# Two-layer encoder on one core: down-stage raw tiles loaded earlier, bank copies moved behind the second step, per-layer input split in the down stage

## The chip, the core and the metric

The kernel runs on one core of one Trainium2 chip. The core has a matrix engine (TensorE, PE below; its weight loads are listed apart as PEld), three engines for elementwise work (VectorE or DVE, ScalarE or ACT, GpSimd or POOL) and SyncE (SP), whose queue issues most of the loads from memory (POOL issues some too). Each engine works through its own queue in order and waits on semaphores for the others. Matmul results stand in eight PSUM banks. The metric is the time of one execution on the device in microseconds (us).

## The reference

Input is a sequence of 512 positions with 1024 features. There are two layers; the parts that the change touches are the feed-forward half-steps and the per-layer input at the end of a layer:

```python
for i in range(DEPTH):                                   # DEPTH = 2
    h = h + 0.5 * swiglu(rmsnorm(h, norm_ffn1[i]), ffn1_w_gate[i], ffn1_w_up[i], ffn1_w_down[i])
    hn = rmsnorm(h, norm_mix[i])
    h = h + (ab_mixer(hn, ...) if i % 2 == 0 else c_mixer(hn, ...))
    h = h + 0.5 * swiglu(rmsnorm(h, norm_ffn2[i]), ffn2_w_gate[i], ffn2_w_up[i], ffn2_w_down[i])
    gate = sigmoid(rmsnorm(h, norm_ple[i]) @ w_ple_gate[i])
    h = h + gate * (p[i] @ w_ple_proj[i])
return rmsnorm(h, norm_final)

# swiglu(x, w_gate, w_up, w_down) = (silu(x @ w_gate) * (x @ w_up)) @ w_down ; hidden width 2816
```

All of it is float32.

## The kernel before

Activations lie with features on the 128 partitions: `h` is 8 tiles of 128 x 512. Every float32 operand of a product is split into a high part (ACT copies it to a rounded type, line 150) and a low part (DVE, at some places POOL, subtracts, line 151); a product is then three matmuls, high x high, high x low, low x high (`mm3`, lines 175 to 177; in the fast products lines 390 to 392 and 498 to 500). So each weight tile goes through a load (`wr`, `rb` or `tmp` tiles), a split on ACT into `wh`, a split on DVE into `wl`, and the matmuls.

One feed-forward half-step (`ffn`, line 420) runs over 22 chunks of 128 hidden features ("pairs" of a gate and an up product). The first five use plain or half-split products, the other 17 (`pair_fast`) seven half-sized ones that are combined on ACT and DVE (lines 399 to 417, the last being the Silu and the product of gate and up). The result is one `act` tile per chunk, in the list `a`.

Then comes the down projection (`down`, line 458), here called a down stage; there are four, starting at about 240, 878, 1285 and 1857 us. It begins with four chunks in plain form on two `tr` banks (`rx`, lines 515 to 519; 24 matmuls). Their raw weights come through `halved`, which takes `tmp` tiles, issues their loads (line 482) and splits them. The two banks are then copied to `act` tiles (`cx`, lines 520 and 506), and two new `tr` banks `rb` are taken. The remaining 18 chunks go in five steps `s` (lines 569 to 573): `first(s)` into two `mm` banks, `second(s)` into an `mm` and the `ob` bank (12 matmuls each, where a step has two chunks), and from the third step on `fifth(s - 2)` into the `sc` banks. Weight sums of two quarters are made by accumulating loads on POOL's queue (line 489). A second loop (lines 590 to 608) runs the rest (`seventh`, `sixth`, `fourth`), and a third the last quarter and the transposes back to `h` with the splits for the next norm.

The per-layer stage (`ple`, line 1331), at about 1000 and 1979 us, loads the two tiles of `p` and splits them (lines 1336 to 1338, low half on POOL), multiplies the first two chunks of the gate and of `p` (`mm_units` and `inner`), starts the third chunk's gate product `ahead`, and then needs the norm's factor R: sums of squares over the partitions by matmuls with ones (line 233, `stat`), scaled on DVE (line 235), raised to -1/2 on POOL (line 236), spread over the partitions by transposes (line 252) and copied by ACT (line 260). With R, DVE frees the gate banks (line 1372).

What sets the order: the program is written in the order above, and at build time a scheduler turns it into one queue per engine, earlier-written work first where its operands and buffers are to be had. Buffers come from pools with fixed counts: 8 `tmp`, 5 `wr`, 2 `rb`, 4 `wh`, 4 `wl`, 62 `act`; of the PSUM banks 3 `mm`, 2 `sc`, 2 `tr`, 1 `ob`. A load stands in SP's queue until its buffer is free, and everything behind it waits with it. `issue_after(ins)` puts the instructions that it encloses behind `ins` on that engine.

Of the kernel before, what the change touches and what calls it, by code (L numbers as in the profile page):

```python
# [16 lines left out]
T = 512  # L17
D = 1024
KC = D // P
# [15 lines left out]
WHOLE = 4  # L35
# [13 lines left out]
class Trunk:  # L49
# [370 lines left out]
    def ffn(self, i, which, k_next):  # L420


        nc, io = self.nc, self.io
        gu, dn = io[f"gu{which}"], io[f"dn{which}"]
        first = i == 0 and which == 1
        a, y, z, t = [], [None] * KC, [None] * (KC // 2), [None] * (KC // 2)

        kept = io["xT"].rearrange("p c t -> c p t") if first else self.put_away()
        xs, sums = [None] * WHOLE, [None] * K2
        for m in range(NF):  # L430
            if m == NF - 1:
                xs[:LEAD_X] = [self.split_chunk(x, nc.vector) for x in a[:LEAD_X]]
            if m < FRONT:
                r = self.pair_front(gu[i, m], m, first, gu[i, m + 1])
            elif m == FRONT:
                r = self.pair(gu[i, m], y, z)
            else:
                r = self.pair_fast(gu[i, m], y, t)
            a.append(r)
            k = (m - WHOLE) // 2  # L440
            if m > WHOLE and (m - WHOLE) % 2 and k < READY:
                sums[k] = self.inner_sums(*a[m - 1:])
            for c, after in enumerate(SUMS):
                if m == after:
                    y[c], z[c], y[c + KC // 2], t[c] = self.halves(c)
        self.begin_norm(k_next)
        self.down(dn[i], a, xs, sums, kept)

    def inner_sums(self, a, b):

# [4 lines left out]
        tt(s[:, l], s[:, r], b[:, r], op=ALU.add)  # L455
        return s

    def down(self, w, a, xs, sums, kept):

        nc, H = self.nc, T // 2
        l, r = slice(0, H), slice(H, T)
# [10 lines left out]
            nc.sync.dma_start(raw, b[:, u.start * T:u.stop * T])  # L474
            return raw

        def halved(b, u):
            hi = self.wh.tile([P, UNIT], F32R, tag="wh", name=self.nm("wh"))
            lo = self.wl.tile([P, UNIT], F32R, tag="wl", name=self.nm("wl"))
            raws = [self.tmp() for _ in u]  # L480
            for raw, k in zip(raws, u):
                nc.sync.dma_start(raw, b[:, k * T:(k + 1) * T])
            for j, raw in enumerate(raws):
                c = slice(j * T, (j + 1) * T)
                self.split(raw, hi[:, c], lo[:, c])
            return hi, lo
# [16 lines left out]
        def copied(p):  # L503
            out = [self.act() for _ in p]
            for o, x in zip(out, p):
                copy(o, x, AF.Copy)
            return out
# [8 lines left out]
        for u in wide:  # L516
            for k in u:
                xs[k] = xs[k] or self.split_chunk(a[k], nc.vector)
            product(rx, u, halved(right, u), xs, r, True, u.stop == WHOLE)
        cx = copied(rx)  # L520
        rb = [self.tbank(), self.tbank()]

        def summed(s):
            raws[s] = load(b12, units[s])
# [13 lines left out]
        def second(s):  # L538
            u = units[s]
            for k in u:  # L540
                x2[k] = self.split_chunk(B[k], nc.vector)
            product(r2, u, halved(b21, u), x2, l, True)
# [26 lines left out]
        for s in range(n):  # L569
            first(s)  # L570
            second(s)
            if s > 1:
                fifth(s - 2)
        c11, c5 = copied(r1), cx
        summed(0)
        seventh(0)
        ws = [halved(left, u) for u in wide]
# [12 lines left out]
        for s in range(1, n + 2):  # L590
            if s + 1 < n:
                summed(s + 1)
            if s < n:
                seventh(s)
            if s <= n:
                sixth(s - 1)
            if s > 1:
                fourth(s - 2)
            if s in (2, 3):
                u = wide[s - 2]  # L600
                product(r3, u, halved(right, u), xs, l)
            if s == n:
                c2 = copied(r1)
                u3 = [self.act(), self.act()]
                for i in range(2):
                    tt(u3[i], c2[i], rb[i], op=sub)
                for i in range(2):
                    tt(c5[i], c5[i], u3[i], op=sub)
# [722 lines left out]
    def ple(self, i, k_next, regroup):  # L1331

        nc, io = self.nc, self.io
        xg, p = self.xg, []
        for c in range(2):
            raw = self.tmp()
            nc.sync.dma_start(raw, io["pT"][i, :, c, :])
            p.append(self.split_chunk(raw))
        up, ends, first = None, [], []
        for m in range(KC):  # L1340
            self.fetch(self.kept, m)
# [5 lines left out]
            if m == 0:  # L1347
                first = [(u, self.bank(), self.obank()), (self.unit(io["plg"][i, 1]), self.bank(), self.sbank())]

                def inner():  # L1350
                    for j, (_, _, q) in enumerate(first):
                        self.mm_unit(q, tuple(x[:, j * 2 * P:(j + 1) * 2 * P] for x in up), p, True, True)

                self.mm_units([f[1] for f in first], [f[0] for f in first], inner)
                next_u, ahead = self.unit(io["plg"][i, 2]), self.bank()
                self.mm_unit(ahead, next_u, xg, True, True)

            half = k_next == N_NORM - 1 and m == KC - 1
            for x in (slice(0, T // 2), slice(T // 2, T)) if half else (slice(0, T),):
# [215 lines left out]
```

## Time and profile before

| | us |
|---|---|
| median of 3 runs | 2052.09 (2049.68 to 2052.36) |
| the profiled execution, on the device | 2050.14 |
| its span from first to last instruction | 2048.4 |
| PE busy | 2008.8 (98%) |
| DVE busy | 1598.8 (78%) |
| ACT busy | 1127.6 (55%) |
| POOL busy | 280.3 (14%) |

The mean granted clock of PE in that execution is 0.994. Times in the rows of the trace count from the span's start. A row of the order of time gives start, duration, engine, line, operation, output and input names (buffer numbers left out), shapes and count, and in brackets how long the engine had been idle and what it had waited for. A matmul's record lasts longer than the interval to the next one, since they are pipelined.

### The profile page before, as it was taken

Reading aid. Unit: us, or ns where it says so; the run is one execution under the profiler, and the core shown is the slowest. Engines: PE = TensorE matmul, PEld = TensorE weight load, DVE = VectorE, ACT = ScalarE, POOL = GpSimd, SP = SyncE. Lnnn points to the kernel's source line nnn. Section 1 sums busy time; section 2 is a strip of 40 time slices with the busy share of each in tenths; the row PEclk is TensorE's granted clock in tenths of the full one; section 3 lists DMA queues with packets and bytes.
Section 4 is the critical chain, followed back from the end, with each engine's and each line's share of the span. In section 5 each row is a group of like instructions: output and inputs, shape, how many; then the busy total and the mean of one; then the engine's idle time right before and its main releaser. Section 6 shows DMA issues by size and latency. Waiting matters only on the chain.

```text
span 2048.4 us, 33392 instructions
## 1 busy us (share of the span) xinstructions
PE 2008.8 (98%) x12438; PEld 1786.9 (87%) x12438; DVE 1598.8 (78%) x2799; ACT 1127.6 (55%) x1954; POOL 280.3 (14%) x318
## 2 busy tenths in 40 slices
PE   9999999999999999999999999999999999999998
PEld 6999888879788899978788999788888889997876
DVE  8888776798766888885778888858888688888675
ACT  6455555477645455564554555745766445556552
POOL 0001011342212000011120000113000200001212
PEclk9999999999999999999999999999999999999998
DMA  6766698553425466588555665985343446657961
GB/s 196 181 183 183 184 205 219 168 95 82 98 62 175 121 186 177 160 218 209 190 165 129 180 182 160 231 206 182 106 128 99 164 117 172 181 165 203 208 227 42
DMA packets 134963, 334.94 MB, mean 164 GB/s; under 512 B 24592, under 2 KB 32272, under 8 KB 134800
## 3 DMA queue, kind: packets, MB, share of 16 engines
q1 hardware_dynamic: 106944, 245.72, 36.2%
q0 software_dynamic: 27712, 87.05, 24.3%
q8 instruction: 98, 1.61, 0.3%
q14 instruction: 65, 0.53, 0.1%
q10 hardware_dynamic: 144, 0.04, 0.0%
HBM read 304.42 MB, written 17.27 MB: 157 GB/s over the span
## 4 chain that ended last, share of the span: by engine, by line
PE 73%; DVE 3%; issue 2%; ACT 2%; POOL 0%; DVEq 0%; ACTq 0%; POOLq 0%
PE mm L176 5%; PE mm L175 5%; PE mm L177 5%; PE mm L392 5%; PE mm L391 5%; PE mm L390 5%; PE sc L391 2%; PE sc L390 2%; PE sc L392 2%; PE mm L498 2%; PE mm L500 2%; PE mm L499 2%; PE sc L177 2%; PE sc L175 2%; PE sc L176 2%
## 5 line engine op out<-in xcount | busy, mean ns | idle before, releaser
L150 ACT ACTIVATE wh<-wr 128x1024 fp32r<-128x1024 f32 (+2 forms) x435 | 448.1, 1032 | 431.1 <-PE mm L176 61.2
L151 DVE TENSOR_TENSOR wl<-wr,wh 128x1024 fp32r<-128x1024 f32 (+2 forms) x435 | 524.0, 1206 | 153.4 <-ACT wh L150 151.7
L391 PE MATMUL mm<-act,wh 128*128 128x256 f32 x1088 | 307.9, 283 | 0.0
L390 PE MATMUL mm<-act,wh 128*128 128x256 f32 x1088 | 307.9, 283 | 0.0
L392 PE MATMUL mm<-act,wl 128*128 128x256 f32 x1088 | 307.9, 283 | 0.0
L175 PE MATMUL mm<-act,wh 128*128 128x512 f32 (+1 forms) x632 | 248.4, 395 | 1.4 <-ACT wh L150 0.6
L176 PE MATMUL mm<-act,wh 128*128 128x512 f32 (+1 forms) x632 | 247.7, 393 | 0.6 <-DVE act L214 0.6
L177 PE MATMUL mm<-act,wl 128*128 128x512 f32 (+1 forms) x632 | 246.9, 391 | 0.9 <-DVE wl L151 0.9
L390 PEld LDWEIGHTS mm<-act,wh 128*128 128x128 f32 x1088 | 208.8, 192 | 0.2
L391 PEld LDWEIGHTS mm<-act,wh 128*128 128x128 f32 x1088 | 208.9, 192 | 0.2
L392 PEld LDWEIGHTS mm<-act,wl 128*128 128x128 f32 x1088 | 208.9, 192 | 0.0
L390 PE MATMUL sc<-act,wh 128*128 128x256 f32 x544 | 154.0, 283 | 0.0
L391 PE MATMUL sc<-act,wh 128*128 128x256 f32 x544 | 154.0, 283 | 0.0
L392 PE MATMUL sc<-act,wl 128*128 128x256 f32 x544 | 154.0, 283 | 0.0
L368 POOL DMA_DIRECT2D wr<-in_gu_dram x68 | 59.2, 870 | 677.4 <-DMA wr<-in_gu_dram 255.8
L175 PEld LDWEIGHTS mm<-act,wh 128*128 128x128 f32 x632 | 119.2, 189 | 25.2 <-ACT wh L150 1.5
L176 PEld LDWEIGHTS mm<-act,wh 128*128 128x128 f32 x632 | 119.3, 189 | 24.9 <-DVE act L214 3.9
L177 PEld LDWEIGHTS mm<-act,wl 128*128 128x128 f32 x632 | 119.1, 188 | 23.2 <-DVE wl L151 1.9
L489 POOL DMA_DIRECT2D wr<-in_dn_dram x80 | 69.3, 879 | 427.8 <-DVE wl L151 220.0
L151 DVE TENSOR_TENSOR act<-act,act 128x512 fp32r<-128x512 f32 (+1 forms) x176 | 108.2, 632 | 13.4 <-ACT act L150 9.4
L150 ACT ACTIVATE act<-act 128x512 fp32r<-128x512 f32 (+1 forms) x176 | 96.9, 577 | 19.5 <-PE sc L500 8.5
L390 PEld LDWEIGHTS sc<-act,wh 128*128 128x128 f32 x544 | 104.4, 192 | 0.0
(255 smaller groups left out, 4888.8 us busy)
## 6 DMA issues: line engine op xcount, KB each, us to landing
wr<-in_gu_dram SPq DMA_DIRECT2D x176, 512.0 KB, 4.4
wr<-in_gu_dram POOLq DMA_DIRECT2D x68, 512.0 KB, 5.5
wr<-in_dn_dram POOLq DMA_DIRECT2D x64, 512.0 KB, 7.5
tmp<-in_dn_dram SPq DMA_DIRECT2D x120, 256.0 KB, 5.1
rb<-in_gu_dram SPq DMA_DIRECT2D x68, 256.0 KB, 2.5
wr<-in_dn_dram SPq DMA_DIRECT2D x32, 512.0 KB, 4.6
act<-kept SPq DMA_DIRECT2D x56, 256.0 KB, 5.3
wr<-in_qk_ab_dram SPq DMA_DIRECT2D x20, 512.0 KB, 3.8
```

Of the source, the lines that this page charges most:

```text
L150: self.put(self.nc.scalar.activation(hi, src, AF.Copy))
L151: self.put((lo_eng or self.nc.vector).tensor_tensor(lo, src, hi.bitcast(F32), op=ALU.subtract))
L175: mm(out, stat[0], mov[0], start=start, stop=False)
L176: mm(out, stat[0], mov[1], start=False, stop=False)
L177: return mm(out, stat[1], mov[0], start=False, stop=stop)
L368: nc.gpsimd.dma_start(rs, w[:, :UNIT], accum_op=ALU.add)
L390: mm(out, w[0][:, c], xs[k][0][:, x], start=start and k == 0, stop=False, skip_group_check=True)
L391: mm(out, w[0][:, c], xs[k][1][:, x], start=False, stop=False, skip_group_check=True)
L392: mm(out, w[1][:, c], xs[k][0][:, x], start=False, stop=stop and k == half - 1, skip_group_check=True)
L489: nc.gpsimd.dma_start(raw, b[:, u.start * T:u.stop * T], accum_op=ALU.add)
L498: mm(p, xh, wh, start=start and k == 0, stop=False, skip_group_check=True)
L499: mm(p, xh, wl, start=False, stop=False, skip_group_check=True)
```

## The change

In `ffn`, ahead of the last pair, four `tmp` tiles (`begin`) are taken and the loads of the first four raw tiles of the down weights are issued; `halved` uses them in place of its own for the `rx` products. In `down`, the copy of the two `rx` banks moves from right behind their products to behind the second step (`s == 1`), and the two new `tr` banks `rb` are taken behind the copy of `r1`, after the loop. In the second half-step of a layer (`which == 2`), `down` calls `inner` in the second turn of its second loop, which loads and splits both tiles of `p`, now with the low half on DVE; `ple` takes them from there. In `ple`, `ahead` is computed in two halves; the sums over the partitions (`rcol`) stand behind the first half and the spread (`R`) behind the second.

```diff
@@ ffn
             if m == NF - 1:
                 xs[:LEAD_X] = [self.split_chunk(x, nc.vector) for x in a[:LEAD_X]]
+                begin = [self.tmp() for _ in range(WHOLE)]
+                for k, raw in enumerate(begin):
+                    nc.sync.dma_start(raw, dn[i, :, (WHOLE + k) * T:(WHOLE + k + 1) * T])
...
-        self.down(dn[i], a, xs, sums, kept)
+        p = lambda: [self.per_layer(i, c) for c in range(2)]
+        self.down(dn[i], a, xs, sums, begin, kept, p if which == 2 else None)
+
+    def per_layer(self, i, c):
+        raw = self.tmp()
+        self.nc.sync.dma_start(raw, self.io["pT"][i, :, c, :])
+        return self.split_chunk(raw, self.nc.vector)
@@ down
-        def halved(b, u):
+        def halved(b, u, raws=None):
...
-            raws = [self.tmp() for _ in u]
-            for raw, k in zip(raws, u):
-                nc.sync.dma_start(raw, b[:, k * T:(k + 1) * T])
+            if raws is None:
+                raws = [self.tmp() for _ in u]
+                for raw, k in zip(raws, u):
+                    nc.sync.dma_start(raw, b[:, k * T:(k + 1) * T])
...
-            product(rx, u, halved(right, u), xs, r, True, u.stop == WHOLE)
-        cx = copied(rx)
-        rb = [self.tbank(), self.tbank()]
+            product(rx, u, halved(right, u, begin[u.start:u.stop]), xs, r, True, u.stop == WHOLE)
...
             second(s)
+            if s == 1:
+                c5 = copied(rx)
             if s > 1:
                 fifth(s - 2)
-        c11, c5 = copied(r1), cx
+        c11 = copied(r1)
+        rb = [self.tbank(), self.tbank()]
...
             if s > 1:
                 fourth(s - 2)
+            if s == 2 and inner:
+                self.p = inner()
@@ ple
-        xg, p = self.xg, []
-        for c in range(2):
-            raw = self.tmp()
-            nc.sync.dma_start(raw, io["pT"][i, :, c, :])
-            p.append(self.split_chunk(raw))
+        xg, p = self.xg, self.p
...
                 next_u, ahead = self.unit(io["plg"][i, 2]), self.bank()
-                self.mm_unit(ahead, next_u, xg, True, True)
+                self.mm_unit(ahead, next_u, xg, True, True, range(KC // 2))
+                with self.tc.issue_after(self.last_mm.ins):
+                    self.rcol
+                self.mm_unit(ahead, next_u, xg, True, True, range(KC // 2, KC))
+                with self.tc.issue_after(self.last_mm.ins):
+                    self.R
```

In the new file the lines behind `ffn` have moved: 498 to 500 are now 509 to 511, 474, 482, 489 and 506 are 484, 493, 500 and 517, and 1372 is 1387. The queues differ from before at the start of the four down stages, in the second loop of two of them, and in the two `ple` stages; elsewhere they are the same. Three places show how, each in the first stage of its kind.

ACT's queue at the end of the last pair and the start of the down stage, before (L408, L414 and L416 belong to the last pair; `act_463` and `act_559` are the third and fourth chunk of `a`, `act_678`, `act_833` and `act_705` operands of the first step):

```order
L416 ACTIVATE act_2721<-act_2721 128x512
L150 ACTIVATE wh_2830<-tmp_2832 128x512
L150 ACTIVATE wh_2830<-tmp_2833 128x512
L150 ACTIVATE wh_2860<-tmp_2862 128x512
L150 ACTIVATE wh_2898<-wr_2888 128x1024
L150 ACTIVATE wh_2860<-tmp_2863 128x512
L150 ACTIVATE wh_2923<-tmp_2925 128x512
L150 ACTIVATE wh_2923<-tmp_2926 128x512
L150 ACTIVATE wh_2955<-wr_2945 128x1024
L506 ACTIVATE act_2882<-tr_2828 128x512
L506 ACTIVATE act_2883<-tr_2829 128x512
L150 ACTIVATE act_2890<-act_678 128x512
```

and now:

```order
L150 ACTIVATE wh_2838<-tmp_2697 128x512
L150 ACTIVATE wh_2838<-tmp_2698 128x512
L150 ACTIVATE act_2856<-act_463 128x512
L150 ACTIVATE act_2860<-act_559 128x512
L150 ACTIVATE wh_2864<-tmp_2699 128x512
L150 ACTIVATE wh_2864<-tmp_2700 128x512
L150 ACTIVATE act_2884<-act_678 128x512
L408 ACTIVATE tmp_2731<-mm_2726 128x256
L150 ACTIVATE act_2888<-act_833 128x512
L150 ACTIVATE wh_2892<-wr_2882 128x1024
L150 ACTIVATE act_2909<-act_705 128x512
L414 ACTIVATE act_2729<-mm_2726 128x256
```

The splits of the four raw tiles and of the first step's operands stand ahead of the last pair's L408 and L414; the bank copies (now L517) stand 13 rows behind the last one shown. DVE's low halves move in the same way.

SP's queue, as a difference (`wr` and `tmp` loads of `in_dn` are raw down weights, `rb_7683` and `rb_7811` belong to a later half-step):

```order
 L366 DMA rb_7683<-in_gu_dram 128x512
-L474 DMA wr_3075<-in_dn_dram 128x1024
-L474 DMA wr_3156<-in_dn_dram 128x512
+L435 DMA tmp_2697<-in_dn_dram 128x512
+L435 DMA tmp_2698<-in_dn_dram 128x512
+L435 DMA tmp_2699<-in_dn_dram 128x512
+L435 DMA tmp_2700<-in_dn_dram 128x512
+L484 DMA wr_3073<-in_dn_dram 128x1024
+L484 DMA wr_3154<-in_dn_dram 128x512
 L366 DMA rb_7811<-in_gu_dram 128x512
-L482 DMA tmp_2832<-in_dn_dram 128x512
-L482 DMA tmp_2833<-in_dn_dram 128x512
```

The four raw tiles now go ahead of two `wr` loads and an `rb` load that they stood behind.

PE's queue in the first `ple` stage around the statistics, before (`mm_11037` is `ahead`, `sc_11113` the third chunk's product with `p`, `mm_11144` the fourth chunk's gate product):

```order
L177 MATMUL mm_11037<-act_10776,wl_11033 128x512
L233 MATMUL tr_11063<-ones,ssq_10903 128x1 x4
L175 MATMUL sc_11113<-act_10935,wh_10956 128x512
L176 MATMUL sc_11113<-act_10936,wh_10956 128x512
L252 MATMUL tr_11072<-ident,rcol_11069 128x128 x4
L177 MATMUL sc_11113<-act_10935,wl_10957 128x512
```

and now, where the ten rows between the two pieces are more of `mm_11037`:

```order
L177 MATMUL mm_11037<-act_10872,wl_11033 128x512
L233 MATMUL tr_11050<-ones,ssq_10915 128x1 x4
L175 MATMUL mm_11037<-act_10746,wh_11032 128x512
...
L177 MATMUL mm_11037<-act_10788,wl_11033 128x512
L252 MATMUL tr_11072<-ident,rcol_11056 128x128 x4
L175 MATMUL sc_11113<-act_10464,wh_10956 128x512
L176 MATMUL sc_11113<-act_10465,wh_10956 128x512
```

Twelve matmuls of `ahead` now stand between the statistics and the spread; the products of the first two chunks with `p` have moved ahead in the queue, among the matmuls on the first gate chunk.

More of the change, by code (lines that the diff above doesn't have):

```diff
@@ L456, in inner_sums, with down @@
         return s
-    def down(self, w, a, xs, sums, kept):
+    def down(self, w, a, xs, sums, begin, kept, inner):
         nc, H = self.nc, T // 2
```

## The prediction

> **What bounds the kernel now.** I read the totals first, then the waits of TensorE (PE), then the order of time around each wait. Totals, and the two longest lines of the waits (engine and line that waited, what released it, us in total, times, longest):
>
> ```profile
> PE 2008.8 (98%) x12438; PEld 1786.9 (87%) x12438; DVE 1598.8 (78%) x2799; ACT 1127.6 (55%) x1954; POOL 280.3 (14%) x318
> ...
> PE tr L498 <- ACT wh L150: 8.5, 4, 2.1
> PE mm L498 <- ACT act L150: 4.8, 4, 1.2
> ```
>
> PE sets the time: the 2048.4 us span gets shorter only where PE's idle or slow time does. Both waits occur four times, once each at the start of the four down stages. The first down stage, in order of time on PE (start, us, engine, line, what; idle before in brackets):
>
> ```profile
> 237.97 0.28 PE L392 MATMUL mm<-act,wl 128*128 128x256 f32 x1
> 240.37 0.80 PE L498 MATMUL tr<-wh,act 128*128 128x512 f32 x1 [2.12 <-ACT wh L150]
> ...
> 247.01 0.39 PE L499 MATMUL tr<-wl,act 128*128 128x512 f32 x1
> 247.24 0.39 PE L500 MATMUL tr<-wh,act 128*128 128x512 f32 x1
> 248.83 0.50 PE L498 MATMUL mm<-wh,act 128*128 128x512 f32 x1 [1.20 <-ACT act L150]
> ```
>
> A 512-column matmul starts every 0.23 us (247.01 to 247.24) though its record lasts 0.39, and a 256-column one every 0.12; an idle time in brackets therefore leaves out 0.16 us of what a wait costs. The entry costs 240.37 - 237.97 - 0.12 = 2.28 us and the second wait 248.83 - 247.24 - 0.23 = 1.36 us. The 24 matmuls between them run from 240.37 to 247.47, 7.1 us, where 24 x 0.23 = 5.5 would do: 1.6 us more. The stretches (us from the start, busy us of PE, PEld, DVE, ACT, POOL; then granted clock, DMA share, GB/s) say why:
>
> ```profile
> 236.80:240.20 3.40, 1.45 (x13) 1.25 (x11) 1.49 (x3) 1.42 (x3) 0.00 (x0) 1.00 0.94 337
> 240.20:243.61 3.41, 3.24 (x8) 2.46 (x9) 3.41 (x6) 3.41 (x7) 0.00 (x0) 0.50 0.56 180
> ...
> 1281.26:1284.67 3.41, 2.05 (x18) 1.85 (x16) 1.17 (x3) 0.83 (x2) 0.00 (x0) 1.00 0.98 348
> 1284.67:1288.08 3.41, 2.58 (x10) 1.86 (x11) 3.19 (x6) 3.41 (x7) 0.00 (x0) 1.00 0.58 189
> ...
> 1015.03:1018.44 3.41, 1.65 (x13) 1.21 (x12) 1.35 (x2) 0.97 (x1) 2.00 (x1) 1.00 0.13 47
> ...
> 1998.06:2001.47 3.41, 3.41 (x11) 2.51 (x10) 1.09 (x2) 2.51 (x3) 0.00 (x0) 0.50 0.00 0
> ```
>
> After such a wait the clock stands at half for one stretch of 3.41 us, which loses 1.7 us of work. There are five such stretches, the first and the last of which are quoted: three down stages and both `ple` stages. The third down stage (1285) had the same wait but its idle fell over two stretches, PE was busy 2.05 us in the first, and the clock stayed at 1.00; 1.65 us busy in the `ple` was too little.
>
> [...]
>
> **Down stages: what the change does.** Why PE enters late: ScalarE (ACT) and the loads on SP's queue.
>
> ```profile
> 235.41 0.38 ACT L408 ACTIVATE tmp<-mm 128x256 f32<-128x256 f32 x1 [2.38 <-PE mm L392]
> ...
> 239.16 0.63 ACT L416 ACTIVATE act<-act 128x512 f32<-128x512 f32 x1 [0.49 <-DVE act L415]
> 239.70 1.65 ACT L150 ACTIVATE wh<-tmp 128x512 fp32r<-128x512 f32 x3
> ...
> 246.99 1.28 ACT L506 ACTIVATE act<-tr 128x512 f32<-128x512 f32 x2 [1.00 <-PE tr L500]
> 248.16 0.62 ACT L150 ACTIVATE act<-act 128x512 fp32r<-128x512 f32 x1
> ```
>
> ```profile
> 222.67 0.33 SPq L366 DMA_DIRECT2D rb<-in_gu_dram  x1
> 227.39 3.90 SPq L474 DMA_DIRECT2D wr<-in_dn_dram  x2
> 232.75 0.33 SPq L366 DMA_DIRECT2D rb<-in_gu_dram  x1
> 233.13 24.56 SPq L482 DMA_DIRECT2D tmp<-in_dn_dram  x18
> ```
>
> The raw tiles are issued from 233.13, behind two `wr` loads and an `rb` load that wait for buffers, and their splits stand on ACT behind the last pair's Silu (239.16), so `wh` is there only at 240.3. In the new order four raw loads follow the `rb` of 222.67 and are issued at some 223 to 225. One lands in 4.6 us (median):
>
> ```profile
> tmp<-in_dn_dram SPq DMA_DIRECT2D x18, 256.0 KB, 4.6
> ```
>
> Four of them behind each other may take twice that, so they are there by 228 to 233. ACT has room for their four splits (three take 1.65 us, 239.70): it idles 2.38 us before the L408 of 235.41, and the `wh` buffers come free as PE works through the pair. **Entry wait: gone, and with it the slow stretch.** The cover is the time between 233 and PE's need at 238.1; gone, the 2.28 us return at each stage.
>
> The second wait has another cause: the two bank copies (L506, 1.28 us on ACT) stand ahead of the split of `act` that PE needs, and they wait for PE's last `tr` matmul. In the new order both splits of the first step stand ahead of the last pair's L414, and the copies some 25 rows later, where their banks have long been ready. **Second wait: gone.** The moved splits cost L408 little: five of 0.5 us now fill its 2.38 us of idle and may hold it some tenths, and PE needs its bank again only after 12 matmuls, 1.4 us later. The copies' banks are next wanted after all five steps, so holding them is free.
>
> What could be late next is VectorE (DVE), which makes the low half of every split and is full early in the stage:
>
> ```profile
> 900.00:910.00 10.00, 10.00 (x46) 8.21 (x45) 10.00 (x20) 6.52 (x12) 2.59 (x3) 1.00 0.85 193
> 920.00:930.00 10.00, 10.00 (x46) 8.29 (x45) 8.46 (x15) 5.67 (x12) 0.86 (x1) 1.00 1.01 288
> ...
> L151 DVE TENSOR_TENSOR wl<-wr,wh 128x1024 fp32r<-128x1024 f32 (+2 forms) x435 | 524.0, 1206 | 153.4 <-ACT wh L150 151.7
> L151 DVE TENSOR_TENSOR act<-act,act 128x512 fp32r<-128x512 f32 (+1 forms) x176 | 108.2, 632 | 13.4 <-ACT act L150 9.4
> ```
>
> One of the first two steps needs six splits of 512 columns and one of 1024: 6 x 0.63 + 1.21 = 5.0 us of DVE against 24 matmuls x 0.23 = 5.5 us of PE. In the new order DVE has done the splits for the `tr` products before the pair ends, and PE then works 5.5 us on those products while DVE works on the first step, so DVE starts about one step ahead and stays there. I take no loss; if the lead does not hold, up to the 1.36 us of the second wait return in each stage.
>
> The sum for one stage: 2.28 + 1.6 + 1.36 = 5.2 us. The third stage has no slow stretch, so 3.6. **Four stages: 3 x 5.2 + 3.6 = 19.2 us.**
>
> **`ple` stages.** Two things move there. First, the per-layer input `p` is loaded and split in the second loop of the down stage, with its low half on DVE. Before, it was split in `ple`, with the low half on POOL; PE, POOL and PE again:
>
> ```profile
> 1000.67 0.50 PE L177 MATMUL mm<-act,wl 128*128 128x512 f32 x1 [0.43 <-DVE wl L151]
> 1005.25 0.50 PE L176 MATMUL ob<-act,wh 128*128 128x512 f32 x1 [0.70 <-POOL act L151]
> ...
> 1001.78 3.42 POOL L151 TENSOR_TENSOR act<-tmp,act 128x512 fp32r<-128x512 f32 x2 [2.86 <-ACT act L150]
> ```
>
> The products with `p` (`ob`, `sc`, 12 matmuls) can now stand ahead of the point of the first wait, which gives DVE 12 x 0.23 = 2.8 us more for the `wl` that was 0.43 late, and the wait on POOL has no cause left. With 0.16 added to each, that takes 0.59 + 0.86 = 1.45 us. The cost, two 0.63 us splits on DVE, two on ACT and two loads on SP's queue, lies beside the first rows of the second loop, at about 930 in the trace of before, where DVE is 8.46 of 10 us busy (920 to 930, above) and PE all of it.
>
> Second, the statistics. The order of time on PE, then ACT, then DVE, and last the same spread at full clock in an FFN stage:
>
> ```profile
> 1014.93 0.95 PE L233 MATMUL tr<-ones,ssq 128*128 128x1 f32 x8
> 1018.21 0.94 PE L252 MATMUL tr<-ident,rcol 128*128 128x128 f32 x4 [1.76 <-POOL rcol L236]
> 1020.65 0.70 PE L175 MATMUL mm<-act,wh 128*128 128x512 f32 x1
> ...
> 1014.94 1.06 ACT L150 ACTIVATE wh<-wr 128x1024 fp32r<-128x1024 f32 x1 [3.65 <-PE mm L176]
> 1019.19 0.60 ACT L260 ACTIVATE R<-tr 128x512 f32<-128x512 f32 x1 [3.19 <-PE tr L252]
> ...
> 1016.03 1.23 DVE L151 TENSOR_TENSOR wl<-wr,wh 128x1024 fp32r<-128x1024 f32 x1
> 1019.82 0.69 DVE L1372 TENSOR_TENSOR tmp<-mm,R 128x512 f32<-128x512 f32 x1 [2.56 <-ACT R L260]
> ...
> 659.78 0.60 PE L252 MATMUL tr<-ident,rcol 128*128 128x128 f32 x4
> 660.14 0.48 PE L175 MATMUL mm<-act,wh 128*128 128x512 f32 x1
> ```
>
> From the statistics (L233) to the spread (L252) the chain over DVE and POOL takes 1018.21 - 1014.93 = 3.28 us. In the new order 12 matmuls of `ahead`, 2.8 us, stand between; with about 0.9 us of L233 itself they fill it, so the wait goes, 1.76 + 0.16 = 1.9 us, and with it the slow stretch, 1.7 us.
>
> **But a new wait comes.** The next `mm` matmul (1020.65) needs a bank that L1372 reads, and L1372 needs R and stands on DVE behind the `wl` of 1016.03. The orders of ACT and DVE at this place are unchanged: ACT's 1.06 us split, which waits for the last `ahead` matmuls, stands ahead of R, and its low half ahead of L1372. Before, both ran under the wait that is now removed. With the spread at time 0 they now run from 0: ACT to 1.06, DVE's `wl` from 1.1 to 2.3, L1372 to 3.0 (R is there by 1.7). PE has for that time the spread (660.14 - 659.78 = 0.36) and six `sc` matmuls (1.4), so it stops from 1.8 to 3.0: 1.2 us, too short by the stretches above to cost clock. **Two stages: 2 x (1.45 + 1.9 + 1.7 - 1.2) = 7.7 us.**
>
> **Sum.** 19.2 + 7.7 = 26.9 us. The first matmul after a wait also takes 0.50 us in place of 0.39 (248.83, 1000.67): 0.11 us at two waits in four stages and three in two, 1.5 us in all. The profiled execution took 2050.1 us (span 2048.4), so 2050.1 - 28.4 = 2021.7; its runs have a median of 2052.1 and reach from 2049.7 to 2052.4. One slow stretch more or less is 1.7 us, most of that spread, and with the waits gone it goes too, so I add nothing for the median. **Predicted: 2021.5 us.**
>
> **Rivals.** (1) *DVE becomes the bound early in the down stage.* For it: DVE is 10.00 of 10 us busy there. Against: PE did not wait once in that stretch although it came out of a wait with nothing prepared. If the second wait returns, 4 x 1.4 = 5.6 us: 2027; if both waits return in full but without the slow clock, 4 x 3.6 = 14.6 us: 2036. (2) *The new wait in `ple` costs clock.* Its place in the 3.41 us stretch is open: PE would be busy about 3.41 - 1.2 = 2.2 us, above the 2.05 that was enough and not far above the 1.65 that was not. With spread and wait of POOL late by some tenths it falls below: 2 x (1.7 + 0.5) = 4.4 us, 2025 to 2026. [...] (3) *No new wait in `ple`*, if ACT or DVE gets its split done earlier than PE's slot release lets me think: 2.4 us less, 2019. (4) *Slower: the raw loads hold up the last pair.* The four splits now stand on ACT ahead of L408, and PE cannot reuse that bank before it. Should the loads land after 235.4, PE stops in the last pair, us for us. To end slower than before, each stage must lose 28.4/4 = 7.1 us on top, so a landing near 243, 18 us after the last issue against 4.6 measured. That the change does not do what it says I exclude by the new order, in which each piece stands where the diff puts it.
>
> **How the numbers follow.** Forecast 0.63, within 2018 to 2024 on its own; rival 1 0.12; rival 2 0.14; rival 3 0.09; rival 4 0.02. The range 2016.5 to 2030 takes in rivals 2 and 3 and the nearer half of rival 1. A change under 0.2% (4 us) cannot be told from none in this kernel. Every case but rival 4 is more than that faster; I leave 0.03 for several small losses together that add up to no change.
>
> **What the profile after will show.** Right: no PE wait at the first `tr` product or at the first `mm` product of the down stages; a granted clock of 1.00 in their first 10 us; the raw loads issued before the pair's last tiles are split; the L517 copies without a PE wait behind them; no POOL split in `ple`; no wait for `rcol`, and in its place one of about 1.2 us of `mm` for DVE's L1387 behind the spread. Wrong: waits of PE on `wl` between 5 and 30 us after the start of a down stage (rival 1), half clock behind the spread (rival 2), an idle PE within the last pair (rival 4), or PE waits in the second loop of the down stages in which `p` is now split.

## The result and the profile after

The changed kernel takes 2018.55 us (median of 4 runs, 2018.03 to 2018.84), against 2051.22 us (2049.68 to 2052.36, 4 runs) for the kernel before on the same chip: a ratio of 0.9841, 95% interval 0.9824 to 0.9858. Its profiled execution took 2018.84 us (span 2017.0), 31.3 us less than the profiled one before (2050.1). The forecast was 2021.5 us with a range of 2016.5 to 2030.

TensorE (PE) is busy for 13.4 us less (2008.8 to 1995.4) in a span that is 31.4 us shorter. Records of matmuls are longer when the clock is at half (with 512 columns 0.63 us in the slow stretch of the first down stage before, 0.39 us right behind it), so the first figure is mostly clock given back; the rest is idle time that went. The totals of the changed kernel:

```profile
PE 1995.4 (99%) x12438; PEld 1782.9 (88%) x12438; DVE 1593.9 (79%) x2803; ACT 1126.0 (56%) x1954; POOL 271.2 (13%) x314
```

The first and the seventh line of its waits of PE (engine, line and what released it, us in total, times, longest):

```profile
PE mm L175 <- DVE tmp L1387: 2.0, 2, 1.0
...
PE tr L252 <- POOL rcol L236: 0.8, 1, 0.8
```

The two lines that led this list before (8.5 and 4.8 us) are gone. The first line is now the wait that the prediction said would be new; the `rcol` wait that is left belongs to the first FFN half-step at the start of the program, which the change does not touch.

**The start of the first down stage after**, in order of time on PE, then SP's queue and one ScalarE (ACT) instruction:

```profile
238.99 0.28 PE L392 MATMUL mm<-act,wl 128*128 128x256 f32 x1
239.11 0.40 PE L509 MATMUL tr<-wh,act 128*128 128x512 f32 x1
239.35 0.40 PE L510 MATMUL tr<-wl,act 128*128 128x512 f32 x1
...
224.07 1.85 SPq L435 DMA_DIRECT2D tmp<-in_dn_dram  x4
...
236.56 0.37 ACT L408 ACTIVATE tmp<-mm 128x256 f32<-128x256 f32 x1
```

Stretches of the same time (busy us of PE, PEld, DVE, ACT, POOL, then granted clock, DMA share, GB/s):

```profile
236.00:240.00 4.00, 4.00 (x32) 3.87 (x31) 4.00 (x8) 3.69 (x8) 0.00 (x0) 1.00 0.97 351
240.00:250.00 10.00, 10.00 (x45) 8.26 (x45) 10.00 (x16) 8.53 (x15) 1.73 (x2) 1.00 0.86 203
```

The first `tr` product follows the last pair's matmul by 0.12 us, the ordinary distance. The four raw tiles are issued at 224.07, in front of the two `wr` loads. PE is busy for every us and the clock stands at 1.00, where before it stood at 0.50 for 3.41 us (240.20 to 243.61). In the PE records, the time by which the distances from start to start exceed the usual one of their shape sums to 5.46, 5.86, 4.28 and 5.88 us in the four stage starts before, and to 0.01 us or less in each after.

**The statistics in the first `ple` stage after**, in order of time on PE, ACT and DVE (VectorE):

```profile
1002.57 0.60 PE L252 MATMUL tr<-ident,rcol 128*128 128x128 f32 x4
...
1004.16 0.40 PE L177 MATMUL sc<-act,wl 128*128 128x512 f32 x1
1005.56 0.50 PE L175 MATMUL mm<-act,wh 128*128 128x512 f32 x1 [1.00 <-DVE tmp L1387]
...
1002.59 1.06 ACT L150 ACTIVATE wh<-wr 128x1024 fp32r<-128x1024 f32 x1 [5.33 <-PE mm L176]
1003.55 0.58 ACT L260 ACTIVATE R<-tr 128x512 f32<-128x512 f32 x1
...
1003.68 1.22 DVE L151 TENSOR_TENSOR wl<-wr,wh 128x1024 fp32r<-128x1024 f32 x1 [3.63 <-ACT wh L150]
1004.82 0.68 DVE L1387 TENSOR_TENSOR tmp<-mm,R 128x512 f32<-128x512 f32 x1
```

And the stretch around the wait:

```profile
1003.40:1006.80 3.40, 2.40 (x10) 1.64 (x10) 2.42 (x3) 2.65 (x4) 0.00 (x0) 1.00 0.24 71
```

No idle is shown in front of the spread (L252) any more. Behind it stands the new wait: R waits on ACT for a weight split of 1.06 us, L1387 on DVE for that split's low half of 1.22 us, and PE for L1387: 1005.56 - 1004.16 - 0.23 = 1.17 us. The clock stays at 1.00.

### The profile page after: what moved, and what is told of

Same layout as the page of the kernel before. It is cut to its first block, busy times and chain, and to the rows that moved or that the text cites. A ratio compares the mean times of both kernels' runs of the same rounds, so it can differ in the third digit from the quotient of the medians.

```text
span 2017.0 us, 33409 instructions
## 1 busy us (share of the span) xinstructions
PE 1995.4 (99%) x12438; PEld 1782.9 (88%) x12438; DVE 1593.9 (79%) x2803; ACT 1126.0 (56%) x1954; POOL 271.2 (13%) x314
## 4 chain that ended last, share of the span: by engine, by line
PE 75%; DVE 3%; ACT 2%; issue 1%; DMA 0%; POOL 0%; DVEq 0%; ACTq 0%; POOLq 0%
PE mm L176 5%; PE mm L175 5%; PE mm L177 5%; PE mm L391 5%; PE mm L392 5%; PE mm L390 5%; PE sc L390 2%; PE sc L392 2%; PE sc L391 2%; PE mm L511 2%; PE mm L509 2%; PE mm L510 2%; PE sc L175 2%; PE sc L177 2%; PE sc L176 2%; PE sc L511 1%
## 5 line engine op out<-in xcount | busy, mean ns | idle before, releaser
L500 POOL DMA_DIRECT2D wr<-in_dn_dram x80 | 69.2, 873 | 405.8 <-DVE wl L151 278.2
```

Source lines behind the costliest of these rows:

```text
L500: nc.gpsimd.dma_start(raw, b[:, u.start * T:u.stop * T], accum_op=ALU.add)
```

## The experiments

The first four kernels do one part of the change each, the others combine or vary parts; each was timed beside the kernel before on its own chip. The first four ran on one chip, where the kernel before took 2051.86 us (2050.08 to 2057.64, 18 runs).

**One part alone: the raw tiles early.**

```diff
@@ ffn, at m == NF - 1 of the kernel before
+                begin = [self.tmp() for _ in range(WHOLE)]
+                for k, raw in enumerate(begin):
+                    nc.sync.dma_start(raw, dn[i, :, (WHOLE + k) * T:(WHOLE + k + 1) * T])
...
@@ down
+            product(rx, u, halved(right, u, begin[u.start:u.stop]), xs, r, True, u.stop == WHOLE)
```

> Only the early raw loads (with the splits that the scheduler then moves ahead); bank copies, p and the ple order as before. Theory 'each wait has its own cause in a queue order': entry wait 0, the slow stretches of three down stages gone, the second wait of 1.2 us (idle as recorded) stays in all four: about 14 us less than before, 2037. Rival 'catch-up' (the entry wait is the time in which ScalarE and VectorE catch up, so it comes back behind the first products): the second wait grows towards 3.5 us, and only the slow stretches, some 5 us, are saved: 2046.

Measured: 2034.36 us (2033.16 to 2036.76, 4 runs), ratio 0.9917 (0.9902 to 0.9931), 17.5 us less. The waits of PE in this kernel:

```profile
PE mm L502 <- ACT act L150: 4.8, 4, 1.2
PE tr L252 <- POOL rcol L236: 4.3, 3, 1.8
```

A stretch of it behind the entry of the first down stage, with the second wait inside:

```profile
240.00:250.00 10.00, 8.80 (x39) 6.89 (x38) 7.93 (x14) 7.88 (x14) 1.21 (x2) 1.00 0.95 223
```

The entry wait is gone in all four stages, the half clock behind it too, and the second wait stands at its old 1.2 us four times, on a 1.00 clock. In the PE records the four starts lose 1.48 us each, 15.6 us less in all than before. So the two waits have causes of their own, and a wait of 1.2 us alone cost no clock in these four places.

**One part alone: the bank copies behind the second step.**

```diff
@@ down of the kernel before
-        cx = copied(rx)
-        rb = [self.tbank(), self.tbank()]
...
             second(s)
+            if s == 1:
+                c5 = copied(rx)
...
-        c11, c5 = copied(r1), cx
+        c11 = copied(r1)
+        rb = [self.tbank(), self.tbank()]
```

> Only the bank copies behind the second step; raw loads, p and the ple order as before. Theory 'own cause': second wait 0, entry wait 2.1 us and the slow stretches stay: about 6 us less, 2045. Rival 'catch-up': with six more splits ahead of the last pair's L408 and L414 the Silu and so the entry are later, the entry wait grows by about what the second loses: within 2 us of before.

Measured: 2049.15 us (2042.46 to 2055.56, 10 runs), ratio 0.9987 (0.9973 to 1.0001), which is not told from none. Its waits of PE:

```profile
PE tr L498 <- ACT wh L150: 8.5, 4, 2.1
PE ob L176 <- POOL act L151: 3.8, 3, 2.4
...
PE tr L499 <- DVE wl L151: 3.3, 4, 0.8
```

PE and DVE at the first down stage in order of time:

```profile
241.28 0.73 PE L498 MATMUL tr<-wh,act 128*128 128x512 f32 x2 [2.12 <-ACT wh L150]
242.84 0.79 PE L499 MATMUL tr<-wl,act 128*128 128x512 f32 x1 [0.83 <-DVE wl L151]
...
240.89 0.69 DVE L151 TENSOR_TENSOR act<-act,act 128x512 fp32r<-128x512 f32 x1
241.49 0.69 DVE L417 SCALAR_TENSOR_TENSOR act<-tmp,act 128x512 f32<-128x512 f32 x1
242.09 1.89 DVE L151 TENSOR_TENSOR wl<-tmp,wh 128x512 fp32r<-128x512 f32 x3
```

The second wait is gone (no L498 wait for `act` is left), but a new one for the tiles' low halves came at every stage. With the copies out of the way, the first step's activation splits stand ahead, and DVE works through them before it reaches the low halves of the late raw tiles at 242.09. What one wait gave, 4 x 1.37 us, the other mostly took back, about 4 x 1.0. The theory that each wait simply goes by itself falls for this part when it stands alone; the rival falls too, since the entry wait did not grow (8.5 us, as before). The second line above also grew (1.4, 2, 0.7 in the kernel before): once, in the second `ple` stage, PE waited 2.4 us for POOL's split of `p`, which hides some of this part's worth in the total.

**One part alone: the per-layer input split early, on VectorE.**

```diff
@@ down, second loop of the kernel before
+            if s == 2 and inner:
+                self.p = inner()
...
@@ ple
-        xg, p = self.xg, []
...
+        xg, p = self.xg, self.p
```

> Only the split of p in the down stage on VectorE; everything else as before. Theory: the waits on POOL (0.7 us recorded) and on wl (0.4) in the two ple stages go, the wait of 1.8 us for rcol and the slow stretch stay: about 3 us less, 2048. Rival: the products with p, done early, no longer fill PE while VectorE makes the last splits of the down stage, and waits of the same size come there: no change.

Measured: 2042.73 us (2042.40 to 2044.53, 4 runs), ratio 0.9958 (0.9943 to 0.9973): 9.1 us, three times what was expected. The wait for POOL's `act` and that for `wl` are gone; the `rcol` wait stays, as expected:

```profile
PE tr L252 <- POOL rcol L236: 4.3, 3, 1.8
```

Two things were underrated. In the PE records, what the waits at `wl` and POOL cost with the late first matmuls around them and two more delays of 0.2 to 0.3 us is some 2.4 us a stage (of which 1.46 is the two waits), 4.7 in both. And the profile shows half clock in only three places, not five: the first down stage and the first `ple` escaped it although their waits of 2.1 and 1.8 us are unchanged. Up to the first down stage this program is the one before, so its escape there does not come from the edit. That it comes from how the run's idle fell against the 3.41 us stretches is my estimate, from the third down stage before, where the idle lay in two stretches (2.05 and 2.58 us busy) and the clock stayed at 1.00. By it, part of this gain, two stretches or some 3.4 us in the profile, is luck of where the waits fell; how much of the medians' 9.1 us is luck stays open.

**One part alone: the split gate unit, statistics between its halves.**

```diff
@@ ple of the kernel before
-                self.mm_unit(ahead, next_u, xg, True, True)
+                self.mm_unit(ahead, next_u, xg, True, True, range(KC // 2))
+                with self.tc.issue_after(self.last_mm.ins):
+                    self.rcol
+                self.mm_unit(ahead, next_u, xg, True, True, range(KC // 2, KC))
+                with self.tc.issue_after(self.last_mm.ins):
+                    self.R
```

> Only the two halves of the product ahead in ple with the statistics between; everything else as before. Theory: the wait for rcol and the slow stretch go in both ple stages, the new wait of about 1.0 us (recorded) for L1387's counterpart comes, the waits on POOL and wl stay: about 5 us less, 2046. Rival: VectorE is late with the sums because POOL's split of p slows it, the statistics wait for it, and the rcol wait stays: at most 2 us less.

Measured: 2048.16 us (2044.09 to 2052.31, 9 runs), ratio 0.9977 (0.9964 to 0.9990): 3.7 us, less than the 5 expected, with runs that spread over 8.2 us. Its waits of PE:

```profile
PE tr L498 <- ACT wh L150: 8.5, 4, 2.1
PE mm L498 <- ACT act L150: 4.8, 4, 1.2
PE mm L175 <- DVE tmp L1377: 2.0, 2, 1.0
```

The `rcol` wait of the two `ple` stages is gone and the new wait stands in its place, alone and of the same size as in the whole change (L1377 is the changed kernel's L1387). It comes from this part. The trace has half clock at neither `ple` stage.

The four parts alone sum to 17.5 + 2.7 + 9.1 + 3.7 = 33.0 us beside 32.7 for the whole. That they agree is partly chance: the second and the fourth gave less than their waits and the third more than its own.

The next four ran together on another chip, the kernel before at 2050.61 us (2049.55 to 2056.83, 9 runs).

**The changed kernel again.** No edit.

> The changed kernel once more, to compare the next three with it on one chip. 2018.5 us, within 1 us of it, since no wait in front of TensorE is left that is long enough to cost clock; if its times spread over 2.7 us or more as those of the kernel before do, the spread did not come from the waits.

Measured: 2019.51 us (2018.21 to 2021.55, 4 runs), ratio 0.9845 (0.9830 to 0.9859). The ratio is that of the first time, but the runs spread over 3.3 us, so the expectation fell. The profiled run was the longest, 2021.55. Stretches of it:

```profile
542.60:546.00 3.40, 3.15 (x26) 2.93 (x25) 3.24 (x13) 2.45 (x9) 0.94 (x2) 0.96 0.72 89
546.00:549.40 3.40, 3.40 (x10) 2.68 (x10) 2.81 (x11) 1.46 (x6) 0.00 (x0) 0.53 0.32 123
...
1395.50:1398.90 3.40, 2.31 (x21) 2.13 (x19) 2.24 (x3) 1.06 (x1) 1.77 (x2) 1.00 0.53 167
1398.90:1402.30 3.40, 3.40 (x18) 3.40 (x18) 1.30 (x2) 0.00 (x0) 1.89 (x1) 0.53 0.26 73
```

The clock went to half twice (0.53 in the rows, since these stretches are cut some 0.2 us off the clock's own), in places that the change does not touch and where the first profile of the changed kernel shows full clock. The first of the two places falls to half in two later traces as well (seven chunks, ten more VectorE instructions). So the change took away waits at which this could happen, not the chance of it.

**The two parts of the down stages together**, `ple` as before: the first two edits above in one kernel.

> The two parts of the down stages together (raw tiles early, bank copies behind the second step), per-layer stage as before. If the parts add up as they measured apart (-17.5 and -2.7 us), 2031.7 us. My theory: the copies alone were worth 2.7 us because with late raw tiles the moved activation splits on VectorE stood ahead of the tiles' low halves and a new wait of 1.0 us came four times; with early raw tiles nothing is late there, so the copies give their whole 4 x 1.37 = 5.5 us on top of the early tiles: 2034.4 - 5.5 = 2028.9 us, with neither the wait on wh at L498, nor that on wl at L499, nor that on act at L502.

Measured: 2030.81 us (2027.85 to 2033.33, 4 runs), ratio 0.9898 (0.9882 to 0.9915). Waits of PE:

```profile
PE tr L252 <- POOL rcol L236: 4.3, 3, 1.8
PE ob L176 <- POOL act L151: 3.8, 3, 2.4
```

No wait is left at the starts of the down stages, neither the old ones nor that for `wl`: with early raw tiles the copies' part costs nothing back. In the PE records each of the four starts loses 0.0 us, where it loses 1.48 us with early tiles alone: 5.9 us, the whole second wait with its late first matmul. The trace decides for the theory. The medians would not: they lie 19.8 us below before, against 20.2 by adding up and 23 by my theory. One reason is the second row: a wait for POOL's split of `p`, 0.7 us in the kernel before, was 2.4 us once, with half clock behind it (records of 0.63 us for 512 columns from 1964.47 on, 0.39 before the wait), as with the copies' part alone. (The spans of the two profiles differ by 5.0 us, 2027.9 to 2032.9, but that contains this wait and one half-clock stretch less.)

**R earlier in `ple`**, to take the new wait away: the spread behind the seventh of eight chunks of the unit ahead, then behind the sixth.

```diff
@@ ple of the changed kernel
-                self.mm_unit(ahead, next_u, xg, True, True, range(KC // 2, KC))
+                self.mm_unit(ahead, next_u, xg, True, True, range(KC // 2, KC - 1))
                 with self.tc.issue_after(self.last_mm.ins):
                     self.R
+                self.mm_unit(ahead, next_u, xg, True, True, range(KC - 1, KC))
```

> The changed kernel with R's four transposes put behind the seventh of the eight chunks of the gate unit computed ahead, not behind the eighth. That puts ScalarE's R copy ahead of the weight split of 1.06 us and VectorE's first L1387 ahead of the split of 1.22 us that it now stands behind. My theory: L1387 ends some 1 us earlier than 1005.5, before TensorE wants the bank at 1004.4, and the new wait of 1.17 us goes in both per-layer stages: 2018.5 - 2.3 = 2016.2 us, faster than the changed kernel. Rival: the two splits put back are late in their turn, or the second L1387 is, and a wait of the same length stands elsewhere in the stage: 2018.5 us.

> The same with the transposes behind the sixth chunk, 0.7 us earlier yet. They would begin at 1001.2, and POOL's rcol ended at 1001.17 in the changed kernel's trace, so they may wait some 0.1 us for it; otherwise as with seven chunks: 2016.3 us if the theory holds, 2018.5 us if the wait only moves.

Measured: with seven chunks 2016.93 us (2015.87 to 2018.56, 4 runs), ratio to the kernel before 0.9832 (0.9817 to 0.9846), and with six 2016.42 us (2015.92 to 2018.92, 5 runs), 0.9834 (0.9819 to 0.9849). In the kernel with seven chunks, no wait of PE for this reader (here L1388) is left; PE, ACT and DVE at that place:

```profile
1005.40 0.39 PE L177 MATMUL sc<-act,wl 128*128 128x512 f32 x1
1005.63 0.40 PE L175 MATMUL sc<-act,wh 128*128 128x512 f32 x1
...
1004.44 0.60 ACT L260 ACTIVATE R<-tr 128x512 f32<-128x512 f32 x1 [5.26 <-PE tr L252]
1004.95 1.06 ACT L150 ACTIVATE wh<-wr 128x1024 fp32r<-128x1024 f32 x1
...
1005.07 0.69 DVE L1388 TENSOR_TENSOR tmp<-mm,R 128x512 f32<-128x512 f32 x1 [3.10 <-ACT R L260]
```

R and the bank's reader now go ahead of the two splits, and nothing new is late. The shortest runs are 2.3 us below the changed kernel's shortest (2015.9 against 2018.2), what 2 x 1.17 says; by medians it is 2.6 and 3.1 us. That is below the 0.2% that these times tell apart, so it is the trace that shows it: in the PE records each `ple` stage loses 1.2 to 1.4 us less. Both are the fastest kernels of this study.

The last three ran together, the kernel before at 2051.42 us (2049.34 to 2053.78, 7 runs).

**More work on VectorE at the start of the down stages**: low halves written again, twice for each of the first step's two tiles in one kernel (below), five times in the other.

```diff
@@ down, first(s) of the changed kernel
                 x1[k] = self.split_chunk(A[k], nc.vector)
+                for _ in range(2 if s == 0 else 0):
+                    nc.vector.tensor_tensor(x1[k][1], A[k], x1[k][0].bitcast(F32), op=ALU.subtract)
```

> The changed kernel with four more VectorE instructions of 0.60 us (the low half of an activation split written again, twice for each of the first step's two tiles) in each of the four down stages: 2.4 us more work there per stage. My theory: at its closest place VectorE ended its half about 2.4 us before TensorE wanted it, so TensorE waits 0 to 0.3 us per stage: 2018.5 to 2020 us, the changed kernel's own time. The rival by which VectorE is already the bound there (my first rival in the prediction): all of it comes out at the end, 4 x 2.4 = 9.6 us, 2028 us or more.

> The same with ten such instructions, 6.0 us more per stage. With a lead of 2.4 us TensorE waits 6.0 - 2.4 = 3.6 us in each of four stages, 14.4 us in all, and a wait of that length costs up to 1.7 us of clock behind it each: 2033 to 2040 us. If VectorE has no lead: 24 us, over 2042 us. If its lead is above 6 us: 2018.5 to 2020 us.

Measured: with four more 2018.04 us (2017.75 to 2020.38, 4 runs), the changed kernel's own time. With ten more 2027.55 us (2027.33 to 2027.87, 4 runs), ratio to the kernel before 0.9883 (0.9869 to 0.9898). That is less than the 2033 us that I expected at least. With ten, the longest line of PE's waits:

```profile
PE mm L511 <- DVE act L545: 3.6, 4, 0.9
```

PE at the first down stage:

```profile
247.29 0.39 PE L510 MATMUL mm<-wl,act 128*128 128x512 f32 x1
248.57 0.73 PE L511 MATMUL mm<-wh,act 128*128 128x512 f32 x2 [0.89 <-DVE act L545]
```

Four cost nothing; of ten, 6.0 us of DVE work, 1.7 us came out on PE in each stage (1.70, 1.71, 1.73 and 1.70 in the PE records of the four starts). VectorE's lead at the first step is thus 6.0 - 1.7 = 4.3 us, not the 2.4 us that I had read off the closest place. The four waits of 0.9 us cost no clock (behind the first one matmuls start every 0.23 us again, 249.14 to 249.37; the mean clock is 0.998, as in the changed kernel). VectorE is full there (10.00 of 10 us in the changed kernel from 240 to 250) and still not the bound.

**The per-layer input split on POOL again, at the new early place.**

```diff
@@ per_layer of the changed kernel
-        return self.split_chunk(raw, self.nc.vector)
+        return self.split_chunk(raw, self.nc.gpsimd)
```

> The changed kernel with the per-layer input's two low halves split on POOL, as in the kernel before, but at the new early place. It tells the place from the engine. My theory: the place alone took the waits away, since POOL's two splits (3.4 us in the kernel before) end some 20 us before TensorE wants them: 2018.5 to 2020 us, nothing lost. The rival: POOL's splits slow VectorE's instructions beside them, as in the kernel before (0.68 to 1.79 us), in a stretch in which VectorE is busy without a break, and TensorE waits for a low half: 2 us or more above.

Measured: 2020.40 us (2019.61 to 2023.18, 4 runs), ratio to the kernel before 0.9851 (0.9836 to 0.9865); its profiled span, 2017.2 us, is that of the changed kernel (2017.0). There is no wait for `p` in `ple`: the place took it away, not the engine. One wait of PE came elsewhere, in the second loop of the first of the two down stages concerned; PE, then POOL's splits, and what led from them to PE on VectorE, POOL and ACT:

```profile
935.01 0.50 PE L510 MATMUL mm<-wl,act 128*128 128x512 f32 x1 [0.67 <-DVE wl L151]
...
920.63 1.62 POOL L151 TENSOR_TENSOR act<-tmp,act 128x512 fp32r<-128x512 f32 x1
922.50 1.94 POOL L151 TENSOR_TENSOR act<-tmp,act 128x512 fp32r<-128x512 f32 x1
...
921.44 4.08 DVE L151 TENSOR_TENSOR wl<-wr,wh 128x1024 fp32r<-128x1024 f32 x1
...
925.82 0.89 POOL L500 DMA_DIRECT2D wr<-in_dn_dram  x1 [1.39 <-DVE wl L151]
...
932.64 1.06 ACT L150 ACTIVATE wh<-wr 128x1024 fp32r<-128x1024 f32 x1 [3.24 <-DMA wr<-in_dn_dram]
```

Beside POOL's splits VectorE's `wl` took 4.08 us, where the same split takes 1.21 us in the changed kernel. The next accumulating load (L500) waits for that `wl` and goes out at 925.82, some 2.8 us later in the stage than in the changed kernel. Its data is what ACT waits 3.24 us for, and PE waits for the low half that follows. So the rival's mechanism, POOL slowing VectorE, did occur; it reached PE at one place, for 0.8 us. The medians differ by some 2 us (2018.04 us for the kernel with four more VectorE instructions, on the same chip), which is below what these times tell apart.

## Why the prediction was right, and by how much each term was off

- **Entry wait, 2.28 us a stage, gone: right.** It is the raw tiles' part alone that does it, and it took the half clock with it, as predicted. The cover held: L408 went to 236.56, 2.55 us ahead of the pair's end, where it had been 2.68 us ahead before (238.09 - 235.41), so the splits ahead of it cost it 0.1 us.
- **Slow clock, 1.6 us in three stages: right in kind, a little small, and its number of places luck.** The records give 1.6 us in the first stage and 2.0 in the second. The third stage, which had no slow stretch, lost 4.28 us where the sum had 3.6 and 0.22 for first matmuls. The four starts lost 21.5 us, against 19.2 + 4 x 0.22 = 20.1 in the sum. Which starts lose clock differs from trace to trace although the entry wait is the same: the first, second and fourth before, the first, third and fourth with the copies' part alone, the second and fourth with `p` alone, the third and fourth with the split gate unit alone. A sum that takes the places from one profile is right for that profile and carries 1.7 us a place beyond it.
- **Second wait, 1.36 us a stage, gone: right, but for a reason that needs the first part.** The prediction costed the two edits side by side. Alone, the copies' part mostly exchanges the wait for one of about 1.0 us on `wl`; with the raw tiles early it gives all of it. (The copies stand 16 and 18 rows behind the two splits, not some 25 as the prediction says; that changes nothing.)
- **VectorE's lead: right.** "I take no loss" held, by 4.3 us. Rival 1 is out: a busy share of 10.00 of 10 says that the engine never rests, not that anyone waits for it.
- **Waits for `wl` and POOL, 1.45 us a `ple` stage: the mis-sized term.** The waits were that long (0.59 and 0.87), but with the late first matmuls and two smaller delays around them, where the sum had 0.11 us a wait, the place lost some 2.4 us. In all, a `ple` stage's lost time went from 6.13 to 1.36 us in the first and from 6.14 to 1.32 in the second: 9.6 us, against 7.7 + 6 x 0.11 = 8.4.
- **The new wait of 1.2 us: right in place, cause and size** (1.17 us). The prediction's schedule from the spread on (split to 1.06, low half to 2.3, L1387 to 3.0) ran as 1.08, 2.33 and 2.93. The sum leaves out the late first matmul behind it, 0.11 us a stage. Rival 3 (no such wait) is out by the trace, although its 2019 us is nearer to the measured time than the forecast; and the kernels with R earlier show that the order behind the wait was its cause.
- **Rival 2 (that wait costs clock): out.** Six traces have this wait in both `ple` stages, and none of the twelve places lost clock (1.00 in the stretch above, 2.40 us of 3.40 busy). The bounds by which the prediction weighed it, 1.65 and 2.05 us busy, do not hold, though (last section).
- **Rival 4 (raw loads hold up the pair): out.** The loads are issued at 224.07, and PE shows no idle in the last pair.
- **Nothing added for the spread of the runs: right in size, but not for its reason.** The gain by medians (32.7 us) and by profiles (31.3) differ by less than one slow stretch, 1.7 us. That the spread goes with the waits held in the first four runs (0.8 us) and not in the next four (3.3 us).

The terms were 28.4 us in all, 20.08 and 8.36; the records give 21.5 and 9.6. The missing 2.6 us are first matmuls after a wait, small delays beside it and a slow stretch that cost 2.0 us in place of 1.6, costs of a wait that its idle time in brackets does not contain.

## What to carry to other kernels

Cost a wait from start to start in the trace, with the slow first matmul (0.50 us in place of 0.39) and the clock behind it (3.41 us at 0.50), not by its idle time: here the idle was a little over half of what went. When a wait is removed, follow what ran unseen beside it on the other engines: splits that nobody waited for became a 1.17 us wait, and moving one reader ahead of them removed that too. And time parts of a change together as well as alone: a reordering that was worth next to nothing with late data was worth its whole wait with early data.

## What the runs showed of the hardware that was not expected

- In one place the clock fell behind a stretch that was nearly full. In the second profile of the changed kernel the stretch at 542.6 has PE busy for 3.15 of 3.40 us, and the next ran at 0.53; its matmuls are short ones (16 of 64x128 in 2.05 us, then 8 of 128x16). PE's longest idle in that stretch is 0.25 us. The first profile of the same kernel has the same instructions (3.14 of 3.40 us busy at 543.3) and a clock of 1.00 there and in the stretch behind.
- The prediction's rule of thumb from one trace, busy time of a stretch between 1.65 us (too little) and 2.05 us (enough), is no rule. Here are two stretches, each with the one behind it, cut on the bounds that the clock keeps in its trace (in the kernel before, the five half-clock stretches begin whole multiples of 3.413 us apart, to 0.01 us): the entry of the first down stage with the split gate unit alone, then the first `ple` stage with the raw tiles alone.

```profile
236.66:240.07 3.41, 1.63 (x14) 1.43 (x12) 1.32 (x3) 1.25 (x3) 0.00 (x0) 1.00 0.95 332
240.07:243.48 3.41, 3.00 (x12) 2.19 (x13) 3.41 (x6) 3.41 (x7) 0.00 (x0) 1.00 0.67 211
...
1006.35:1009.76 3.41, 2.18 (x14) 1.62 (x12) 1.35 (x2) 1.06 (x1) 1.53 (x1) 1.00 0.23 85
1009.76:1013.17 3.41, 2.88 (x9) 2.26 (x10) 0.69 (x1) 1.71 (x2) 0.48 (x1) 0.50 0.46 154
```

  After 1.63 us the clock stayed, after 2.18 it fell; the latter holds the eight 128x1 matmuls of the statistics, 0.95 us of records. An estimate from the traces fits better: count a matmul of 512 columns as 0.227 us, the usual distance to the next, and one of fewer columns in proportion. Then the stretches ahead of all 23 half-clock ones in the 13 traces (their first 7 and last 12 us aside) hold 0.45 to 1.41 us, whether their matmuls are short or long, and only ten of some 7,600 others hold so little, the lowest 1.14. By this count the new wait in `ple` leaves 1.98 us or more. It is a fit and no test, and what decides between 1.1 and 1.4 us is open.
- VectorE and POOL took longer beside each other, and it was not always the same one. In the kernel before, a VectorE sum that takes 0.68 us elsewhere took 1.79 us beside POOL's splits, which took 3.42 us for the two. In both kernels that move the copies and leave `p` on POOL, the first split in the second `ple` stage took 4.03 us in place of some 1.72 (5.7 us for the two), VectorE's instructions beside it their usual 0.69 and 1.22 us, and PE waited 2.4 us. In each case POOL began some 0.65 us into a VectorE split (1001.78 - 1001.14 and 1981.24 - 1980.59 in the kernel before), so that does not decide which one takes longer; what does, no run shows.
